# Order of a planned kernel: how many waiting tiles of the big pool a tile may pass, 2 to 6, and result stores without a due time

## The chip, the cores and the metric

The kernel runs on one core of one Trainium2 chip. Times are device microseconds (us) of one execution, as the device measures it; the median of the runs counts. Beside the timed runs there is one execution that the hardware profiler recorded, with each engine's instructions: TensorE (PE, matmuls), VectorE (DVE), ScalarE (ACT), GpSimd (POOL) and SyncE (SP, which issues DMAs).

## The reference

One layer of a streaming encoder on x of 1024 positions by 1024 channels, in float32. Cut to what matters:

```python
h = x @ w_in + b_in                      # 1024 x 6144
xa, za, xb, zb, ga, gb = split(h)        # six of 1024 channels
ya = rg_lru(causal_conv4(xa)) * silu(za) # gates by 16 blocks of 64x64, then a scan over time
yb = multi_scale_pool(xb) * silu(zb)     # running means over 2, 4, 8, 16 steps, then 4 blocks of 256x256
merged = sigmoid(ga) * (ya @ w_proj_a) + sigmoid(gb) * (yb @ w_proj_b)
x = layer_norm(2**0.25 * x + merged @ w_out + b_out) * gain + bias
```

In the scan, `h_t = a_t * h_{t-1} + u_t`, with `a = exp(-8 * r * softplus(-lambda))`: a vector softplus(-lambda) of 1024 numbers is needed once, before the first gate's exponential.

## The kernel before

**Tiling.** All is laid out with channels on the 128 partitions and time along the free axis. Each float32 operand of a matmul is split into a rounded high part (a cast on ACT) and the rest (a subtraction on DVE), and three matmuls of 128x512 (high by high, high by low, low by high) stand for one product: names end in `h` and `l`. The large products are done by a seven-product block scheme after Strassen and Winograd, whose sums of blocks DVE makes, or DMAs that add.

**Stages, by the trace's time.** From 0 to about 60 us a first part loads x and the first weights and does the groups `G0` and `A0` in an order of its own: the sums of x blocks are `t13`, `t24` (one buffer each for four quarters), their high and low parts are `x13h`, `x57h`, `x64h` and `x64l`, `xp0` is the first input of the convolution, and the softplus is a chain of DVE instructions on 128x8 with one exponential on ACT in it (lines 1070 to 1092, tiles `sp_y`, `sp_z`, `sp_z2`, `sp_acc`). From 60 to 404 us the groups A1, G2, A2, ... alternate: a group A makes eight channels' worth of xa and za, and its convolution `xc`, its split into `xch` and `xcl`, gates `ps_g`, `r`, `i`, and the scan follow two groups later. Then the groups B (xb, zb, pooling products `ps_pool`) until 511 us. From 511 to 675 us the merge: a list of 14 steps (`steps`, line 1164: a1, a2, a6, a5, a3, a7, a4, then b1, b2, b6, b7, b5, b4, b3), each four output tiles of twelve matmuls; the last pool product stands before a3. In step i the operands of step i+1 are cast (`cast`, line 1180: raw tiles such as `xb3r0`, `wb3r1` of step 13 become `oh13_0` to `oh13_3` on ACT and `ol13_0` to `ol13_3` on DVE) and those of step i+2 loaded (`load`, line 1170). What a step ends is multiplied by a gate, added into `m00`, `m20`, `m40`, ... and split on ACT and DVE (`split_m`, line 1213: `m000`, `m040` are high parts, `m100` low ones). From 675 us the last product `ps_o`, then the norm and the stores.

**What sets the order.** The code above only records tasks. `Plan.order` (line 253) then plays the kernel through with a table of costs and gives every task a start; the instructions are emitted in the order of these starts, all from line 387. PE and POOL keep the order in which the code records them; DVE, ACT and SP take, of the tasks whose inputs are there in the play, the one with the earliest due time, and the due time follows from when PE would need the result. What a task writes into must have a buffer: tiles with the same tag share a pool's buffers (`x`: 28 buffers of 128x1024, which hold x, its sums, and in the merge the `oh` and `ol`, gates and `m`; `w` 10, `r` 4, `k` 10, `e` 4). `slots` (line 282) hands them out in the order in which the code first writes the tiles, except that a tile may take a buffer ahead of some that still wait: it must stand among the first `AHEAD_OF[tag]` of the waiting tiles, and only if enough buffers are free for those ahead of it too. An SP task (a DMA) may not start earlier than 25 us before its due time (`LEAD`, line 36). On the chip each engine runs its instructions strictly in the order emitted, each when its semaphores allow.

Of the kernel before, what the change touches and what calls it, by code (L numbers as in the profile page):

```python
# [35 lines left out]
LEAD = 25.0  # L36
# [1 line left out]
SOON = 2.0  # L38
SHORT = ("ps", "e")
SHORT_LATEST = 1.0  # L40
AHEAD_OF = {"k": 6, "e": 2, "gr": 1, "x": 2}


C_BIN = 0
# [117 lines left out]
class Plan:  # L162
# [90 lines left out]
    def order(self):  # L253
        T = self.tasks
        for t in T:
            for j in t.deps:
                T[j].users.append(t.i)
        clock, pos = 1.5, []
        ideal = {}
        for t in T:  # L260
            if t.eng == "PE":
                ideal[t.i] = clock
                clock += t.time
            pos.append(clock)
        for t in reversed(T):
            short = t.eng != "PE" and any(r.tile.tag in SHORT for r in t.ins)
            t.due = ideal.get(t.i, pos[t.i] + (SHORT_LATEST if short else t.late))
            for u in t.users:
                t.due = min(t.due, T[u].due - t.wait)
        tags = {}  # L270
        for t in T:
            t.left, t.ready, t.start = len(t.deps), 0.0, None
            for s in t.new:
                if s.left == 0:
                    s.left = len(s.users)
                    tags.setdefault(s.tag, ([0.0] * s.pool.bufs, []))[1].append(s)
        free = {e: 0.0 for e in ("PE", "DVE", "ACT", "POOL", "SP")}
        waiting = {e: [] for e in free}
        pe = [t for t in T if t.eng == "PE"]
        state = {"table": None, "SP": 0.0, "POOL": 0.0, "pe": 0}  # L280

        def slots(t, now, commit=False):

            when = now
            for s in t.new:
                if not s.held:
                    times, queue = tags[s.tag]
                    ahead = queue.index(s)
                    if ahead >= AHEAD_OF.get(s.tag, 1) or len(times) <= ahead:
                        return None  # L290
                    when = max(when, sorted(times)[ahead])
                    if commit:
                        s.held = True
                        queue.remove(s)
                        times.remove(max((x for x in times if x <= now), default=min(times)))
            return when

        def begin(t, now):
            slots(t, now, True)
            if t.table and state["table"] not in t.table:  # L300
                now += 1.29
                state["table"] = min(t.table)
            t.start = now
            free[t.eng] = now + t.time
            if t.dma:
                state[t.eng] = max(now + t.time + 1.2, state[t.eng]) + t.dma
                t.end = state[t.eng] + 0.7
            else:
                t.end = now + t.wait
            for u in t.users:  # L310
                u = T[u]
                u.left -= 1
                u.ready = max(u.ready, now + t.time if u.eng == t.eng and not t.dma else t.end)
                if u.left == 0 and u.eng != "PE":
                    waiting[u.eng].append(u)
            for r in {x.tile: x for x in t.outs + t.ins}:
                r.left -= 1
                r.end = max(r.end, t.end)
                if r.left == 0 and r.tag and not r.pool.dram:
                    tags[r.tag][0].append(r.end)  # L320

        for t in T:
            if t.left == 0 and t.eng != "PE":
                waiting[t.eng].append(t)
        now, done = 0.0, 0
        while done < len(T):
            moved = True
            while moved:
                moved = False
                while state["pe"] < len(pe) and pe[state["pe"]].left == 0:  # L330
                    t = pe[state["pe"]]
                    when = slots(t, max(free["PE"], t.ready))
                    if when is None:
                        break
                    begin(t, when)
                    state["pe"] += 1
                    done += 1
                    moved = True
                for e in ("ACT", "DVE", "SP", "POOL"):
                    if free[e] > now:  # L340
                        continue
                    can, soon = [], []
                    for t in waiting[e]:
                        if t.chain is not None and T[t.chain].start is None:
                            continue
                        when = slots(t, max(now, t.ready, t.due - LEAD if e == "SP" else 0.0))
                        if when is None:
                            continue
                        if when <= now:
                            can.append(t)  # L350
                        elif when < now + 3.0:
                            soon.append((when, t))
                    if e == "ACT":
                        key = lambda t: (t.due + (SWITCH if t.table and state["table"] not in t.table else 0.0), t.i)
                    else:
                        key = lambda t: (t.due, t.i)
                    for t in sorted(can, key=key):
                        end = now + t.time + (1.29 if t.table and state["table"] not in t.table else 0.0)
                        if any(u.due < t.due and when < end and u.due < end - HOLD for when, u in soon):
                            continue  # L360
                        waiting[e].remove(t)
                        begin(t, now)
                        done += 1
                        moved = True
                        break
            times = [f for f in free.values() if f > now]
            for e in waiting:
                for t in waiting[e]:
                    if t.chain is not None and T[t.chain].start is None:
                        continue  # L370
                    when = slots(t, max(t.ready, t.due - LEAD if e == "SP" else 0.0))
                    if when is not None and when > now:
                        times.append(when)
            if done < len(T):
                if not times:
                    raise RuntimeError("stuck at %.1f: %s" % (now, [(t.op, t.args[0].tile.name if isinstance(t.args[0], Ref) else "", t.i) for e in waiting for t in waiting[e]][:20] + [[(k, len(v[0]), [s.name for s in v[1][:3]]) for k, v in tags.items()], T[pe[state["pe"]].i].args[0].tile.name]))
                now = min(times)
        return sorted(T, key=lambda t: (t.start, t.i))
# [21 lines left out]
def layer_kernel(ctx: ExitStack, tc: tile.TileContext, xq, x, w_in, par, wg, w_pool, wpa, wpb, w_out, rows, out):  # L400
# [206 lines left out]
    def load_group(i):  # L607
        w = weights_steps(i)
        for js in ("4", "75", "63 apart", "12") if i >= len(order) - 2 else ("12", "4", "75", "63"):
            w.step(js)  # L610
        return w.out
# [488 lines left out]
    weight_sums("a", wpa)  # L1100
    weight_sums("b", wpb)
    for i in range(1, len(order)):
        kind, c = order[i]
        if i + 1 < len(order):
            W[i + 1] = load_group(i + 1)
# [322 lines left out]
```

## Time and profile before

| | us |
|---|---|
| median of 3 runs (769.88, 773.46, 773.16) | 773.16 |
| the profiled execution | 771.97 |
| its span (first to last instruction) | 770.2 |
| PE busy | 749.9 |
| DVE busy | 602.6 |
| ACT busy | 432.4 |

A view of one engine's instructions in time gives for each row the start, the length, the engine, the line, the operation, what it writes and reads, and, in brackets, how long the engine was idle just before and whose result it waited for. Buffer numbers are left out of names there: `ol` stands for `ol9_1` as for `ol13_3`. Since line 387 emits everything, the line tells nothing; time and names do. Successive matmuls overlap: a row may be 0.39 long and the next starts 0.23 later. The granted clock (PEclk) is the share of full speed at which TensorE was let run in a stretch: 1.00 is 2.4 GHz, and the other of its two levels is 1.2 GHz.

### The profile page before, as it was taken

What the parts mean: (1) busy time and instruction counts of PE and PEld (TensorE: products, weight loads), DVE (VectorE), ACT (ScalarE), POOL (GpSimd) and SP (SyncE); (2) the same over time, 40 slices, a digit from 0 to 9 for tenths busy, and PEclk for the clock granted to TensorE, in tenths of its full rate; (3) what the DMA queues carried; (4) which work ended last, traced back from release to release, by engine and by line L of the source; (5) the groups of instructions that cost most, each with busy time, mean ns of one, the idle gap of its engine ahead of it and who ended that gap; (6) DMA issues with size and microseconds to landing.
All of it is one profiled execution on the core that took longest, in us unless ns stands there. A gap on an engine that the chain in (4) does not pass through costs nothing.

```text
span 770.2 us, 8752 instructions
## 1 busy us (share of the span) xinstructions
PE 749.9 (97%) x3308; PEld 610.6 (79%) x3308; DVE 602.6 (78%) x768; ACT 432.4 (56%) x556; POOL 36.3 (5%) x74
## 2 busy tenths in 40 slices
PE   8989999999999999999999999999999999899996
PEld 5868888888888888888878888888888877688885
DVE  5999686969696969696898678679658968978487
ACT  6657868777777868686755354464452655230000
POOL 0001010000000101000001101000000100000000
PEclk9989999999999999999999999999999999999998
DMA  8235764666476658352219849795699995262022
GB/s 300 86 112 151 202 165 139 184 170 167 178 176 166 168 162 218 132 178 82 69 54 206 152 123 255 247 323 198 219 295 304 339 288 185 91 251 104 27 84 110
DMA packets 54731, 135.91 MB, mean 176 GB/s; under 512 B 3936, under 2 KB 7136, under 8 KB 54624
## 3 DMA queue, kind: packets, MB, share of 16 engines
q1 hardware_dynamic: 41792, 99.69, 37.1%
q0 software_dynamic: 12896, 35.65, 21.3%
q8 instruction: 26, 0.43, 0.2%
q14 instruction: 17, 0.14, 0.0%
HBM read 114.36 MB, written 56.62 MB: 222 GB/s over the span
## 4 chain that ended last, share of the span: by engine, by line
PE 86%; DVE 9%; ACT 2%; DMA 1%; issue 1%; SPq 0%; DVEq 0%; ACTq 0%
PE ps_o L387 11%; PE a_A L387 10%; PE a_G L387 10%; PE a_B L387 7%; PE pa_a L387 6%; PE c_A L387 6%; PE pa_b L387 5%; PE c_G L387 5%; PE c_B L387 4%; PE ps_pool L387 3%; PE e_A L387 3%; PE pc_a L387 3%; PE pc_b L387 2%; PE e_G L387 2%; PE ps_s L387 2%; PE e_B L387 2%
## 5 line engine op out<-in xcount | busy, mean ns | idle before, releaser
L387 PE MATMUL ps_o<-woh,m 128*128 128x512 f32 (+1 forms) x272 | 80.3, 379 | 0.0
L387 ACT ACT_TABLE_LOAD x39 | 50.0, 1283 | 39.9 <-DVE mv L387 38.5
L387 PEld LDWEIGHTS ps_o<-woh,m 128*128 128x128 f32 x272 | 50.1, 188 | 9.9
L387 PE MATMUL ps_o<-wol,m 128*128 128x512 f32 (+1 forms) x136 | 51.5, 379 | 0.0
L387 DVE TENSOR_TENSOR i<-i,xc 128x1024 f32<-128x1024 f32 x8 | 9.8, 1226 | 45.3 <-ACT i L387 45.3
L387 DVE SCALAR_TENSOR_TENSOR xc<-xp,par_sb,xc 128x1024 f32<-128x1024 f32 x24 | 30.8, 1283 | 0.5
L387 PEld LDWEIGHTS ps_o<-wol,m 128*128 128x128 f32 x136 | 25.6, 188 | 4.9
L387 ACT ACTIVATE m<-m 128x512 fp32r<-128x512 f32 x16 | 9.8, 628 | 30.7 <-DVE m L387 30.7
L387 PE MATMUL pa_b<-oh,oh 128*128 128x512 f32 x64 | 25.1, 392 | 1.7 <-ACT oh L387 1.7
L387 PE MATMUL pa_b<-oh,ol 128*128 128x512 f32 x64 | 25.3, 395 | 0.5 <-DVE ol L387 0.5
L387 PE MATMUL pa_b<-ol,oh 128*128 128x512 f32 x64 | 25.1, 392 | 0.7 <-DVE ol L387 0.7
L387 DVE TENSOR_TENSOR z<-ps_o,z 128x512 f32<-128x512 f32 (+1 forms) x17 | 11.2, 659 | 17.9 <-PE ps_o L387 17.4
L387 PE MATMUL pa_a<-oh,ol 128*128 128x512 f32 x64 | 24.9, 389 | 0.0
L387 PE MATMUL pa_a<-oh,oh 128*128 128x512 f32 x64 | 24.9, 389 | 0.0
L387 PE MATMUL pa_a<-ol,oh 128*128 128x512 f32 x64 | 24.9, 389 | 0.0
L387 POOL COPY paced<-pace 128x1 f32<-128x1 f32 x19 | 8.3, 435 | 341.8 <-ACT pace L387 341.8
L387 ACT ACTIVATE r<-ps_g,par_sb 64x512 f32<-64x512 f32 x32 | 21.9, 683 | 2.5 <-PE ps_g L387 2.0
L387 PE MATMUL c_A<-x64h,wd_A 128*128 128x512 f32 x64 | 22.7, 417 | 0.0
L387 ACT ACTIVATE i<-ps_g,par_sb 64x512 f32<-64x512 f32 x32 | 21.9, 683 | 0.5
L387 ACT ACTIVATE sd<-mv,eps 128x1 f32<-128x1 f32 x8 | 2.4, 294 | 34.8 <-DVE mv L387 34.8
L387 PE MATMUL ps_pool<-mixh,wp 128*128 128x512 f32 x64 | 21.9, 415 | 0.0
L387 ACT ACTIVATE zb<-zb,par_sb 128x1024 f32<-128x1024 f32 (+1 forms) x16 | 14.9, 937 | 11.6 <-DVE zb L387 11.4
(434 smaller groups left out, 2378.0 us busy)
## 6 DMA issues: line engine op xcount, KB each, us to landing
sg<-sg SPq DMA_DIRECT2D x16, 512.0 KB, 3.5
ra_A<-in_w_in SPq DMA_DIRECT2D x8, 512.0 KB, 5.7
rb_A<-in_w_in SPq DMA_DIRECT2D x8, 512.0 KB, 4.3
ya<-r SPq DMA_DIRECT2D x8, 512.0 KB, 2.9
ra_B<-in_w_in SPq DMA_DIRECT2D x8, 512.0 KB, 3.4
rb_B<-in_w_in SPq DMA_DIRECT2D x8, 512.0 KB, 4.3
yb<-zb SPq DMA_DIRECT2D x8, 512.0 KB, 6.0
sgla<-sg SPq DMA_DIRECT2D x8, 512.0 KB, 7.6
```

The source lines that it names most:

```text
L387: getattr(getattr(nc, t.op[0]), t.op[1])(*a, **k)
```

## The change

Three lines of the planner. Of the tiles that wait for a buffer of the pool `x`, a tile that stands among the first six may now take one, where it was the first two. And DMAs whose result no other task reads are no longer held to 25 us before their due time; of all DMAs only the 16 stores of the result are such.

```diff
-AHEAD_OF = {"k": 6, "e": 2, "gr": 1, "x": 2}
+AHEAD_OF = {"k": 6, "e": 2, "gr": 1, "x": 6}
...
-                        when = slots(t, max(now, t.ready, t.due - LEAD if e == "SP" else 0.0))
+                        when = slots(t, max(now, t.ready, t.due - LEAD if e == "SP" and t.users else 0.0))
...
-                    when = slots(t, max(t.ready, t.due - LEAD if e == "SP" else 0.0))
+                    when = slots(t, max(t.ready, t.due - LEAD if e == "SP" and t.users else 0.0))
```

No instruction is added or taken away. PE and POOL keep their order row for row; DVE, ACT and SP are ordered anew in many places, the DMAs of SP only from its 109th row on (the loads of the merge), and the 16 stores of the result stand at the same rows as before. Three places:

**The softplus in the first part, on DVE** (`nps` is a small constant made in both; `sp_y` is the exponential that ACT writes; `xp0` reads the product `e_A0`). Before:

```order
L387 TENSOR_SCALAR nps_372<-par_sb_154 128x8
L387 SCALAR_TENSOR_TENSOR xp0_103<-e_A0_354,par_sb_154,m1_A0_358 128x512
L387 TENSOR_TENSOR wcl_A0_385<-ra_A0_125,wch_A0_374 128x1024
L387 SCALAR_TENSOR_TENSOR t24_0_393<-t13_0_225,xr0_0_87 128x512
L387 SCALAR_TENSOR_TENSOR t24_1_400<-t13_1_234,xr1_0_100 128x512
L387 SCALAR_TENSOR_TENSOR t24_2_407<-t13_2_312,xr2_0_113 128x512
L387 TENSOR_SCALAR sp_z_414<-sp_y_369 128x8
L387 RECIPROCAL sp_z_414<-sp_z_414 128x8
L387 TENSOR_TENSOR sp_z_414<-sp_z_414,sp_y_369 128x8
```

The same place of the changed kernel:

```order
L387 TENSOR_SCALAR nps_374<-par_sb_154 128x8
L387 TENSOR_SCALAR sp_z_378<-sp_y_326 128x8
L387 RECIPROCAL sp_z_378<-sp_z_378 128x8
L387 TENSOR_TENSOR sp_z_378<-sp_z_378,sp_y_326 128x8
L387 TENSOR_TENSOR sp_z2_383<-sp_z_378 128x8
L387 TENSOR_TENSOR sp_acc_98<-sp_acc_98,sp_z2_383 128x8
L387 TENSOR_SCALAR sp_acc_98<-sp_acc_98 128x8
...
L387 SCALAR_TENSOR_TENSOR xp0_103<-e_A0_357,par_sb_154,m1_A0_359 128x512
L387 TENSOR_TENSOR wcl_A0_397<-ra_A0_125,wch_A0_376 128x1024
L387 SCALAR_TENSOR_TENSOR t24_0_404<-t13_0_176,xr0_0_87 128x512
```

Nine of the chain's instructions, from the first that reads `sp_y` on, have moved from behind three sums `t24` to ahead of `xp0`; of the 13 that stood between the sum `t24_3` and the next `x64l0`, 11 are left.

**A turn of the A and G groups, on DVE** (`xc1` the convolution, `xcl1` its low part that the gate product reads, `xp2` the next group's input, which reads the product `e_A2`). Before:

```order
L387 TENSOR_TENSOR wbl_A2_959<-rb_A2_717,wbh_A2_941 128x1024
L387 SCALAR_TENSOR_TENSOR xc1_944<-xp1_599,par_sb_154,xc1_944 128x1024 x2
L387 TENSOR_TENSOR sg32_6_982<-c_G2_892,u2_G2_955 128x512
L387 TENSOR_TENSOR sg32_6_982<-a_G2_853,m7_G2_912 128x512
L387 SCALAR_TENSOR_TENSOR r0_756<-a0_832,i0_770 128x1024
L387 TENSOR_TENSOR xcl1_1012<-xc1_944,xch1_980 128x1024
L387 TENSOR_TENSOR ra_A2_676<-ra_A2_676 128x512
L387 MEMSET xp2_1022 128x3
L387 SCALAR_TENSOR_TENSOR xp2_1022<-e_A2_1007,par_sb_154,m1_A2_1009 128x512
L387 TENSOR_TENSOR r0_756<-r0_756,z0_530 128x1024
L387 TENSOR_TENSOR wcl_A2_1041<-ra_A2_676,wch_A2_1025 128x1024
```

The same place of the changed kernel:

```order
L387 MEMSET xp2_969 128x3
L387 TENSOR_TENSOR sg32_6_973<-c_G2_892,u2_G2_953 128x512
L387 TENSOR_TENSOR wbl_A2_978<-rb_A2_717,wbh_A2_959 128x1024
L387 TENSOR_TENSOR ra_A2_684<-ra_A2_684 128x512
L387 TENSOR_TENSOR sg32_6_973<-a_G2_847,m7_G2_912 128x512
L387 SCALAR_TENSOR_TENSOR xc1_945<-xp1_589,par_sb_154,xc1_945 128x1024 x2
L387 TENSOR_TENSOR r0_756<-r0_756,z0_540 128x1024
L387 SCALAR_TENSOR_TENSOR xp2_969<-e_A2_1010,par_sb_154,m1_A2_1012 128x512
L387 TENSOR_TENSOR xcl1_1037<-xc1_945,xch1_1018 128x1024
L387 TENSOR_TENSOR wcl_A2_1044<-ra_A2_684,wch_A2_989 128x1024
```

`xcl1` has moved from ahead of `xp2`, with the scan `r0<-a0,i0` before it, to right behind `xp2`; the scan now stands further up. The like is found in each of the seven turns.

**The end of the merge, on ACT** (`oh13_0` to `oh13_3` are the four high parts of the last step, b3; `m041`, `m040`, `m060` are high parts of results of step b4 and before it, which wait for DVE's sums). Before:

```order
L387 ACTIVATE m041_5155<-m41_4576 128x512 x2
L387 CAST oh12_3_5177<-wb4r1_4978 128x1024
L387 CAST oh13_0_5189<-xb3r0_5046 128x1024
L387 ACTIVATE m040_5200<-m40_4703 128x512
L387 CAST oh13_1_5204<-xb3r1_5070 128x1024
L387 CAST oh13_2_5218<-wb3r0_5145 128x1024
L387 ACTIVATE m040_5200<-m40_4703 128x512
L387 ACTIVATE m060_5265<-m60_4733 128x512
L387 CAST oh13_3_5269<-wb3r1_5193 128x1024
```

The same place of the changed kernel:

```order
L387 CAST oh12_3_5094<-wb4r1_4983 128x1024
L387 ACTIVATE m041_5138<-m41_4583 128x512
L387 CAST oh13_0_5144<-xb3r0_4994 128x1024
L387 ACTIVATE m041_5138<-m41_4583 128x512
L387 CAST oh13_2_5168<-wb3r0_5098 128x1024
L387 CAST oh13_1_5175<-xb3r1_5015 128x1024
L387 CAST oh13_3_5203<-wb3r1_5120 128x1024
L387 ACTIVATE m040_5213<-m40_4692 128x512 x2
L387 ACTIVATE m060_5253<-m60_4786 128x512
```

`oh13_3` has moved up past two `m040` and one `m060`. **In step b2, on DVE** (`ol9_0` to `ol9_3` are the low parts for step b6; `m1_b0` to `m1_b3` its results on their way into `m00` and `m20`). Before:

```order
L387 TENSOR_TENSOR m1_b1_4748<-m1_b1_4748,sglb2_0_4719 128x512
L387 TENSOR_TENSOR m00_4175<-m00_4175,m1_b1_4748 128x512
L387 SCALAR_TENSOR_TENSOR m100_4864<-m00_4175,m000_4847 128x512
L387 TENSOR_TENSOR m1_b2_4776<-pe_b2_4851,m1_b2_4776 128x512
L387 SCALAR_TENSOR_TENSOR ol9_2_4876<-wb6r0_4612,oh9_2_4822 128x1024
L387 TENSOR_TENSOR m1_b2_4776<-m1_b2_4776,sglb2_1_4721 128x512
L387 TENSOR_TENSOR m20_4214<-m20_4214,m1_b2_4776 128x512
L387 TENSOR_TENSOR m1_b3_4807<-pe_b3_4870,m1_b3_4807 128x512
L387 TENSOR_TENSOR ol9_1_4900<-xb6r1_4690,oh9_1_4812 128x1024
L387 TENSOR_TENSOR m1_b3_4807<-m1_b3_4807,sglb2_1_4721 128x512
L387 TENSOR_TENSOR m20_4214<-m20_4214,m1_b3_4807 128x512
L387 SCALAR_TENSOR_TENSOR ol9_3_4915<-wb6r1_4636,oh9_3_4878 128x1024
```

The same place of the changed kernel:

```order
L387 TENSOR_TENSOR ol9_0_4771<-xb6r0_4626,oh9_0_4736 128x1024
L387 TENSOR_TENSOR m60_4786<-um_a2_4304,sgla4_1_4606 128x512
L387 TENSOR_TENSOR m60_4786<-um_a3_4325,sgla4_1_4606 128x512
L387 TENSOR_TENSOR ol9_1_4799<-xb6r1_4633,oh9_1_4782 128x1024
L387 SCALAR_TENSOR_TENSOR ol9_2_4821<-wb6r0_4577,oh9_2_4814 128x1024
L387 TENSOR_TENSOR m1_b0_4745<-pe_b0_4824,m1_b0_4745 128x512
L387 TENSOR_TENSOR m1_b0_4745<-m1_b0_4745,sglb2_0_4641 128x512
L387 TENSOR_TENSOR m00_4181<-m00_4181,m1_b0_4745 128x512
L387 TENSOR_TENSOR m1_b1_4773<-pe_b1_4845,m1_b1_4773 128x512
```

`ol9_1` and `ol9_2` have moved up from among the instructions on `m1_b2` and `m1_b3` to ahead of all on `m1_b0`. The casts of the earlier steps have moved in the same direction.

## Rows read from the trace of the kernel before

**Rows 1.** Page, engines: busy us (share of the span) and instructions.

```profile
PE 749.9 (97%) x3308; PEld 610.6 (79%) x3308; DVE 602.6 (78%) x768; ACT 432.4 (56%) x556; POOL 36.3 (5%) x74
```

**Rows 2.** PE's waits by what was awaited: us in total, times, longest.

```profile
PE a_A L387 <- DVE x64l L387: 3.1, 1, 3.1
PE ps_pool L387 <- DVE mixl L387: 2.6, 2, 1.9
```

**Rows 3.** Busy us by engine (PE, PEld, DVE, ACT, POOL) and PEclk, by stretch.

```profile
50.00:75.00 25.00, 25.00 (x97) 20.06 (x98) 23.60 (x39) 15.22 (x19) 2.35 (x3) 0.88 0.51 168
60.00:400.00 340.00, 340.00 (x1534) 277.44 (x1533) 271.21 (x317) 254.50 (x323) 21.91 (x36) 1.00 0.54 155
```

**Rows 4.** PE in time, first part: start, length, operation, idle before.

```profile
49.86 0.80 PE L387 MATMUL a_A<-x64l,wch_A 128*128 128x512 f32 x1 [3.10 <-DVE x64l L387]
50.88 0.63 PE L387 MATMUL c_A<-x64h,wd_A 128*128 128x512 f32 x1
```

**Rows 5.** DVE in time, first part.

```profile
36.44 0.75 DVE L387 SCALAR_TENSOR_TENSOR xp<-e_A,par_sb,m_A 128x512 f32<-128x512 f32 x1 [1.20 <-PE e_A L387]
...
40.04 0.17 DVE L387 TENSOR_SCALAR sp_z<-sp_y 128x8 f32<-128x8 f32 x1
...
44.78 0.16 DVE L387 TENSOR_TENSOR sp_acc<-sp_acc,sp_z 128x8 f32<-128x8 f32 x1
...
47.23 0.17 DVE L387 TENSOR_TENSOR sp_acc<-sp_acc,sp_z 128x8 f32<-128x8 f32 x1
...
49.12 0.69 DVE L387 TENSOR_TENSOR x64l<-t,x64h 128x512 fp32r<-128x512 f32 x1
```

**Rows 6.** ACT in time, first part.

```profile
33.65 0.59 ACT L387 COPY m_A<-a_A 128x512 f32<-128x512 f32 x1 [0.43 <-PE a_A L387]
...
36.23 1.28 ACT L387 ACT_TABLE_LOAD   x1
...
37.52 0.21 ACT L387 ACTIVATE sp_y<-sp_y 128x8 f32<-128x8 f32 x1
```

**Rows 7.** DVE in time, one turn of groups A and G.

```profile
115.46 1.20 DVE L387 TENSOR_TENSOR xcl<-xc,xch 128x1024 fp32r<-128x1024 f32 x1
...
118.17 0.75 DVE L387 SCALAR_TENSOR_TENSOR xp<-e_A,par_sb,m_A 128x512 f32<-128x512 f32 x1 [0.89 <-PE e_A L387]
```

**Rows 8.** PE in time, the same turn.

```profile
121.04 0.40 PE L387 MATMUL ps_g<-xcl,gh 64*128 64x512 f32 x2
```

**Rows 9.** PE in time, merge.

```profile
616.17 0.39 PE L387 MATMUL pa_b<-oh,oh 128*128 128x512 f32 x1
617.23 0.50 PE L387 MATMUL pa_b<-ol,oh 128*128 128x512 f32 x1 [0.67 <-DVE ol L387]
...
655.45 0.50 PE L387 MATMUL pc_b<-oh,ol 128*128 128x512 f32 x1 [0.80 <-DVE ol L387]
...
668.06 0.50 PE L387 MATMUL pa_b<-oh,oh 128*128 128x512 f32 x1 [1.71 <-ACT oh L387]
...
669.32 0.50 PE L387 MATMUL pa_b<-oh,ol 128*128 128x512 f32 x1 [0.52 <-DVE ol L387]
```

**Rows 10.** DVE in time, merge.

```profile
615.96 1.21 DVE L387 TENSOR_TENSOR ol<-xb6r,oh 128x1024 fp32r<-128x1024 f32 x1
...
654.18 1.22 DVE L387 TENSOR_TENSOR ol<-wb4r,oh 128x1024 fp32r<-128x1024 f32 x1
```

**Rows 11.** ACT in time, merge.

```profile
650.10 0.63 ACT L387 ACTIVATE m<-m 128x512 fp32r<-128x512 f32 x1 [7.74 <-DVE m L387]
...
666.45 0.63 ACT L387 ACTIVATE m<-m 128x512 fp32r<-128x512 f32 x1 [2.85 <-DVE m L387]
666.98 1.03 ACT L387 CAST oh<-wb3r 128x1024 fp32r<-128x1024 f32 x1
```

**Rows 12.** SP's issues in time, merge.

```profile
602.66 0.36 SPq L387 DMA_DIRECT2D xb7r<-t3b  x1
```

**Rows 13.** The tile xb7r: its loads' time to landing.

```profile
DMA to landing us min/median/max: 12.7/13.2/13.6
```

## The prediction

> **What bounds the kernel now.** The page's engine rows come first: PE is busy for 749.9 of the 770.2 us of the span, DVE for 78% of it [rows 1]. PE's matmuls are the same before and after, in the same order, so the time can only move by PE's idle stretches, by the granted clock, and by the head and the tail. The list of PE's waits says which idle stretches there are. The largest is one of 3.1 us for an `x64l` from DVE, in the first part; pooling products wait 2.6 us in two places [rows 2]. The others that matter lie in the merge, four of them, and PE's rows there show each: 0.67, 0.80, 1.71 and 0.52, together 3.70 us [rows 9]. Each costs more than its bracket, since the first matmul after it is 0.50 long, where the one before it is 0.39 (616.17 and 617.23 in [rows 9]): 4 x 0.11 = 0.44. The merge's waits are thus worth 4.1 us. Between 60 and 400 us PE is busy throughout, at full clock [rows 3]. So the change can win 4.1 us in the merge, may win or lose in the first part, and can only lose in the groups.
>
> The wait in the first part has a second price. After it the granted clock is down: 0.88 is the mean of 50 to 75 us [rows 3], and matmuls take 0.63 [rows 4]. With two levels, 1.2 and 2.4 GHz, a mean of 0.88 over 25 us is (1 - 0.88) x 2 x 25 = 6 us at the lower level. The engine had been idle for 3.10 us before that.
>
> **The second edit** frees the 16 stores of the result from their due time, and none of them changes its row on SP. It costs and gives nothing.
>
> **First part: cost 0.85 us.** DVE stands still for 1.20 us before `xp0` at 36.44 [rows 5]. The planner now puts nine instructions of the softplus there. On the chip they cannot run there: they read `sp_y`, which ACT writes. ACT's copy of m1 starts at 33.65 and takes 0.59; its table load for the exponential takes 1.28 and the exponential 0.21 [rows 6]. In the changed order these three follow each other at once, so `sp_y` is there at 33.65 + 0.59 + 1.28 + 0.21 = 35.7 (37.7 before). The chain's step is (47.23 - 44.78) / 12 = 0.204 [rows 5], so nine take 1.84, and `xp0`, behind them, starts at about 35.8 + 1.84 = 37.7 instead of 36.44: 1.26 late. From there to the `x64l` for which PE waits, DVE has the same work but two chain steps fewer (11 instead of 13 before `x64l0`): -0.41. That `x64l` then starts at 49.12 + 0.85 = 49.97 [rows 5], and PE waits 0.85 longer. Nothing hides it: PE is waiting there already.
>
> How the clock takes a longer wait is shown by no row. From below: the low stretch ends at the same moment, then 0.85 us less of it falls on matmuls, which gives back half, and the cost is 0.4. From above: the low stretch lasts half as long again, 3 us more, half of which is lost, and the cost is 0.85 + 1.5 = 2.4. I take the same 6 us, as after the wait that is there, and keep 0.4 to 2.4.
>
> One rule speaks for a higher cost. In the trace the exponential starts at 37.52, and the table load before it ends at 36.23 + 1.28 = 37.51 [rows 6]: nothing lies between. The Trainium skill, page "ScalarE: Activation LUTs", section "What ACT_TABLE_LOAD costs", gives 1283 ns for the load and about 1380 ns more for a drain with each switch. The first figure agrees with the row, the second this row does not show; by it the first part would cost about 2.2 us (an estimate from that page) and the whole come to 771.5.
>
> **Groups A and G: no cost.** In each of seven turns `xcl`, the low part that the gate product reads, now stands behind the next `xp` instead of ahead of it. That `xp` waits for PE (0.89 before it) and starts at 118.17; `xcl` follows 0.68 later, at 118.85, and takes 1.20: done at 120.05 [rows 7]. The matmul that reads it starts at 121.04 [rows 8]. It has 1.0 us to spare. The scan, which now stands further up, gives DVE the time to have the rest of the convolution done before that `xp`.
>
> **Pooling: nothing.** Around both pooling waits [rows 2] the order is as before.
>
> **Merge: -4.1 us, and 0.2 back.** All four waits have one form: a cast or a low part for the next step stands behind instructions that finish the present one. The first is for `ol9_1`, 615.96 to 617.17, and the second for `ol12_3`, 654.18 to 655.40 [rows 10]. `ol12_3` was late because its high part on ACT stands behind `m041`, which waited 7.74 us for DVE's sum until 650.10. `oh13_3` is the worst: it starts at 666.98 behind `m060` at 666.45, which again waited for DVE [rows 11], and PE's third and fourth waits are for it and for its low part. In the new order `ol9_1` and `ol9_2` stand ahead of all the evacuations of step b2, and `oh13_3` ahead of `m040` and `m060`. Since casts of the steps before also move up, raw buffers come free earlier and SP's loads go out earlier. `oh12_3` can be cast where ACT falls idle, at 650.10 - 7.74 = 642.4 [rows 11], 9.5 us sooner, so `ol12_3` is there about 10 us before PE wanted it (655.45 - 0.80 = 654.65, [rows 9]). Walking on with the durations of before, the raw buffer that `ol12_3` frees gets `wb3r1` soon after, `oh13_3` is cast at about 650, and `ol13_3` is ready at about 656, 10 us before PE first stood still for it (668.06 - 1.71 = 666.35, [rows 9]). Four waits gone: -4.1.
>
> What comes next is a chain on ACT in step b6. The cast `oh10_0` now stands ahead of `m000`, and has to wait for the load of `xb7r`; that load is behind an addition by DMA that no reordering moves, takes 12.7 to 13.6 us to land [rows 13], and the second was issued at 602.66 [rows 12], so the data can be there only at about 602.66 + 13.2 = 615.9. Behind it on ACT come `m000` and `oh10_1`, then on DVE `m100`, m1_b3 and `ol9_3`, and by my walk `ol9_3` ends 0.7 to 2 us before PE wants it. Bounds: 0 if the landing is like the median, 2.4 us if it is two low parts (1.21 each, [rows 10]) late. I take 0.2, near the lower end.
>
> The product with w_out and the tail keep their order: nothing.
>
> **Sum,** against the profiled execution: 771.97 + 0.85 - 4.1 + 0.2 = 768.9. That execution was 1.19 below the median of the runs (773.16), so in the frame of the median: 770.1.
>
> **The rivals.**
>
> *Waits for loads take the place (C).* The chain on ACT above is late by the whole 2.4 us. For it: the loads of `xb7r` land late and spread over 0.9 us. Against it: it was not late before, and the casts ahead of it are done earlier. 770.1 - 0.2 + 2.4 = 772.3.
>
> *The table switch takes longer than its row (T).* Something as long as the load itself (1.28, [rows 6]) lies between load and exponential once the exponential follows a copy directly. Against it: 37.51 to 37.52. 770.1 + 1.28 = 771.4. The drain that the Trainium skill gives on the page named above would be such a thing.
>
> *The change does not do what it says (D).* A buffer that the planner believes free is free later on the chip, casts in the new order wait for loads as long as they waited for sums, and the four waits stay; the first part still pays. For it: the planner's DMA times are a model, and DMAs are dense in this stretch. Against it: two of the four waits are behind sums on ACT, in front of which the casts now stand, with their raw tiles long landed. 773.16 + 0.85 + 0.2 = 774.2.
>
> *The groups pay seven times (E), slower than before.* `xcl` has 1.0 us to spare in my walk. If two more instructions of its size (1.20, [rows 7]) come between `xp` and `xcl` in time, because the scan or the product with the silu is done later than I have it, each turn loses 2.4 - 1.0 = 1.4: 770.1 + 7 x 1.4 = 779.9. The kernel becomes slower than 773.16 from 0.44 us a turn on, that is, with `xcl` 1.5 us later than I have it. For it: seven copies of one margin. Against it: DVE stood still before that `xp`, so up to there it has slack.
>
> **How the numbers follow.** A measurement of this kernel tells about 0.5% from no change, 3.9 us: faster is below 769.3, slower above 777.0. Forecast 0.66; C 0.09; T 0.04; D 0.10; E 0.11. The forecast lies 0.8 above the bound for faster, and the unknown terms (first part 0.4 to 2.4, chain 0 to 2.4) and the runs' own spread (769.88 to 773.46) put it on either side, half and half: 0.33 faster, 0.33 same. C, T and D are within 0.5%: same 0.33 + 0.09 + 0.04 + 0.10 = 0.56; slower is E, 0.11. The range: below, the forecast less 2.7, as a run as far under the median as most of the spread (773.16 - 769.88 = 3.3) would give: 767.4. Above, D with 0.6 for its spread: 774.8. Outside lie E and some 0.06 of the rest.
>
> **What would show it.** In the trace after: the wait for `x64l` is 3.9 to 4.0 us instead of 3.1, and `xp0` starts at 37.7 with `sp_y` as what it was held by; PEclk of 50 to 75 stays at 0.86 to 0.88. PE's waits for `oh` and `ol` in the merge are below 0.5 us together; the pooling waits stay at 2.6. `xcl` of a turn ends at least 0.5 us before its matmul. I am wrong in the merge if waits for `oh` or `ol` remain near 617, 655 or 667, or a new one stands near 620 to 626 (C); wrong in the groups if `ps_g` appears among PE's waits, seven times (E); wrong in the first part if the wait for `x64l` is over 5 us or PEclk of 50 to 75 below 0.83.

## The result, and the profile after

The changed kernel takes 765.47 us in the median (765.15 to 767.53), the one before 772.63 in the same comparison: a ratio of 0.9921, 95% interval 0.9897 to 0.9945. That is 7 us, where 3 were forecast, and below the low end of the range (767.4). The profiled execution took 765.47, with a span of 763.7, against 771.97 and 770.2 before: 6.5 us less.

PE's waits by what was awaited, kernel after (us in total, times, longest):

```profile
PE a_A L387 <- DVE x64l L387: 3.3, 1, 3.3
PE ps_pool L387 <- DVE mixl L387: 2.6, 2, 1.9
...
PE c_A L387 <- DVE x64l L387: 0.9, 1, 0.9
```

Against [rows 2], the first wait is 3.3 instead of 3.1 (3.9 to 4.0 were forecast), the pooling waits are the same 2.6, and a second wait for an `x64l` of 0.9 is new. No wait for an `oh` or `ol` is left: the merge's four waits [rows 9] are gone.

Since PE's instructions stand in the same order, the start of the same matmul in both traces tells where time was won. The table gives the first matmul of a block in each; the last column is what changed since the row above.

| start of the block | before | after | after less before | step |
|---|---|---|---|---|
| a_A, first part | 30.73 | 30.89 | +0.16 | +0.16 |
| a_G, after the waits for x64l | 56.20 | 56.50 | +0.30 | +0.14 |
| a_B, after the first pooling product | 409.27 | 408.01 | -1.26 | -1.56 |
| pc_b of step b7 | 626.66 | 624.35 | -2.31 | -1.05 |
| pa_b of step b3 | 660.57 | 656.99 | -3.58 | -1.27 |
| ps_o | 674.45 | 667.88 | -6.57 | -2.99 |

The merge gives 5.3 us, the first part costs 0.14, and 1.56 come from a place where the wait has not changed. The first step, 0.16, says nothing: over the 14 profiled executions of this document that block starts anywhere from 29.9 to 30.9, over the four of the kernel before from 30.2 to 30.9. Busy time by stretch shows what it is (columns as in [rows 3]: PE, PEld, DVE, ACT, POOL, then PEclk). Kernel before:

```profile
400.00:425.00 25.00, 23.12 (x95) 18.48 (x94) 20.23 (x28) 13.94 (x18) 3.22 (x3) 0.93 0.83 193
650.00:675.00 25.00, 21.96 (x94) 17.00 (x93) 23.04 (x33) 9.46 (x13) 0.00 (x0) 1.00 0.39 126
```

Kernel after:

```profile
50.00:75.00 25.00, 23.59 (x96) 19.09 (x97) 23.08 (x33) 15.21 (x19) 2.35 (x3) 0.93 0.51 169
400.00:425.00 25.00, 23.12 (x101) 18.68 (x100) 20.88 (x29) 14.81 (x19) 3.17 (x3) 1.00 0.79 187
650.00:675.00 25.00, 25.00 (x111) 20.63 (x110) 23.74 (x37) 9.12 (x13) 0.00 (x0) 1.00 0.19 58
```

After the first pooling wait the granted clock was 0.93 before and is 1.00 now, with PE's busy time equal (23.12): the wait stayed, the low clock behind it did not come. In 50 to 75 us the clock is 0.93, not the 0.88 of [rows 3] or the 0.86 to 0.88 that was forecast. In 650 to 675 us PE is busy throughout, where it had 21.96 of 25.

The first part, DVE after, which answers to [rows 5]:

```profile
35.94 0.17 DVE L387 TENSOR_SCALAR sp_z<-sp_y 128x8 f32<-128x8 f32 x1 [1.55 <-ACT sp_y L387]
...
37.69 0.75 DVE L387 SCALAR_TENSOR_TENSOR xp<-e_A,par_sb,m_A 128x512 f32<-128x512 f32 x1
...
49.79 0.69 DVE L387 TENSOR_TENSOR x64l<-t,x64h 128x512 fp32r<-128x512 f32 x1
...
55.19 0.68 DVE L387 TENSOR_TENSOR x64l<-t,x64h 128x512 fp32r<-128x512 f32 x1
```

ACT after, which answers to [rows 6]:

```profile
33.81 0.59 ACT L387 COPY m_A<-a_A 128x512 f32<-128x512 f32 x1 [1.77 <-PE a_A L387]
34.40 1.28 ACT L387 ACT_TABLE_LOAD   x1
35.70 0.21 ACT L387 ACTIVATE sp_y<-sp_y 128x8 f32<-128x8 f32 x1
```

The chain's first reader of `sp_y` starts at 35.94, `xp0` at 37.69, both within 0.15 of the prediction (35.8, 37.7). The `x64l` that PE waits for starts at 49.79, 0.67 later than before, where 0.85 were forecast; 0.16 of it is there already at a_A.

A turn of the groups after, which answers to [rows 7, 8], DVE and then PE:

```profile
118.45 0.75 DVE L387 SCALAR_TENSOR_TENSOR xp<-e_A,par_sb,m_A 128x512 f32<-128x512 f32 x1 [1.17 <-PE e_A L387]
119.12 1.22 DVE L387 TENSOR_TENSOR xcl<-xc,xch 128x1024 fp32r<-128x1024 f32 x1
```

```profile
121.33 0.39 PE L387 MATMUL ps_g<-xcl,gh 64*128 64x512 f32 x2
```

`xcl` ends at 119.12 + 1.22 = 120.34, 1.0 us ahead of its matmul, as worked out.

The merge after, DVE and then ACT, which answers to [rows 10, 11]:

```profile
599.57 1.23 DVE L387 TENSOR_TENSOR ol<-xb6r,oh 128x1024 fp32r<-128x1024 f32 x1
...
638.76 1.22 DVE L387 TENSOR_TENSOR ol<-wb4r,oh 128x1024 fp32r<-128x1024 f32 x1
...
655.08 1.22 DVE L387 TENSOR_TENSOR ol<-wb3r,oh 128x1024 fp32r<-128x1024 f32 x1
```

```profile
605.98 1.05 ACT L387 CAST oh<-xb7r 128x1024 fp32r<-128x1024 f32 x1 [0.23 <-DMA xb7r<-t3b]
...
610.04 1.05 ACT L387 CAST oh<-xb7r 128x1024 fp32r<-128x1024 f32 x1 [1.72 <-DMA xb7r<-t3b]
...
646.63 1.05 ACT L387 CAST oh<-wb3r 128x1024 fp32r<-128x1024 f32 x1
```

`ol9_1` is done at 600.8 (617.2 before), `ol12_3` at 640.0 (655.4), `oh13_3` at 647.7 (668.0) and `ol13_3` at 656.3 (669.3). ACT does wait for the loads of `xb7r`, 0.23 and 1.72 us, as the rival C had it; PE does not feel it.

The second edit: with it alone, and two tiles to pass, the order of all five engines is row for row that of before; with the first edit alone it is that of the changed kernel. So it has no part in the result.

### The profile page after: what moved, and what is told of

It is laid out like the page before. It is cut to its first block, busy times and chain, and to the rows that moved or that the text cites. A ratio compares the mean times of both kernels' runs of the same rounds, so it can differ in the third digit from the quotient of the medians.

```text
span 763.7 us, 8776 instructions
## 1 busy us (share of the span) xinstructions
PE 746.5 (98%) x3308; PEld 609.3 (80%) x3308; DVE 603.7 (79%) x768; ACT 433.9 (57%) x556; POOL 37.7 (5%) x74
## 4 chain that ended last, share of the span: by engine, by line
PE 87%; DVE 9%; DMA 1%; ACT 1%; issue 1%; SPq 1%; DVEq 0%
PE ps_o L387 12%; PE a_G L387 10%; PE a_A L387 10%; PE a_B L387 9%; PE pa_b L387 6%; PE pa_a L387 6%; PE c_A L387 5%; PE c_G L387 5%; PE c_B L387 4%; PE pc_a L387 3%; PE pc_b L387 3%; PE ps_pool L387 3%; PE e_B L387 2%; PE e_A L387 2%; PE e_G L387 2%; PE ps_g L387 2%
## 5 line engine op out<-in xcount | busy, mean ns | idle before, releaser
L387 PEld LDWEIGHTS ps_o<-wol,m 128*128 128x128 f32 x136 | 25.6, 188 | 5.0
L387 PE MATMUL c_B<-x64h,wd_B 128*128 128x512 f32 x64 | 21.0, 389 | 0.0
```

What stands on the lines that cost most here:

```text
L387: getattr(getattr(nc, t.op[0]), t.op[1])(*a, **k)
```

## The experiments

Times before are given as measured beside each group of runs: 771.99 (23 executions) for the first four, 771.95 for the next four, 771.68 for the last four. What a ratio's interval means in us is worked out with these.

**The two kernels once more.** Nothing is edited; the question is the granted clock.

> The kernel before once more, unchanged, for the granted clock. Theory A (the low-clock stretches fall differently in each execution): PE's waits are the same within 0.2 us, but the stretch after the first pooling wait (400 to 425 us) or the one after the wait for x64l (50 to 75 us) comes out at another clock than in the first profile (0.93 and 0.88), and the times spread over 2 to 4 us in steps of about 1.7. Theory B (the clock follows from the order of the instructions): both stretches come out as in the first profile within 0.01, and the times spread by under 1 us.

> The changed kernel once more, unchanged. Theory A: the first pooling wait is again followed by a stretch at the lower clock in some executions (0.93 in 400 to 425 us instead of 1.00), times from 765 to 768. Theory B: 1.00 in 400 to 425 us and 0.93 in 50 to 75 us again. In both: no wait for oh or ol in the merge.

Before again: 772.33 (771.17 to 774.07, 12 executions). After again: 765.60 (764.45 to 766.85), ratio 0.9916 (0.9899 to 0.9933), 6.5 us. In the merge and at the pooling products PE's waits are those of the first two profiled executions; in the first part the kernel before now has a second wait for `x64l`, of 1.0, which its first profiled execution did not have. The clock differs too. The kernel before, second profiled execution, by stretch:

```profile
400.00:425.00 25.00, 23.11 (x102) 18.85 (x102) 20.90 (x29) 14.31 (x18) 3.02 (x3) 1.00 0.85 203
665.00:670.00 5.00, 3.72 (x9) 2.71 (x10) 4.22 (x6) 2.39 (x4) 0.00 (x0) 0.69 0.01 3
```

The low clock after the pooling wait is missing here as it is in the kernel after; instead there is one in the merge. PE there:

```profile
665.76 0.50 PE L387 MATMUL pa_b<-oh,oh 128*128 128x512 f32 x1 [1.71 <-ACT oh L387]
...
667.01 0.80 PE L387 MATMUL pa_b<-oh,ol 128*128 128x512 f32 x1 [0.52 <-DVE ol L387]
667.61 0.63 PE L387 MATMUL pa_b<-oh,oh 128*128 128x512 f32 x1
668.03 0.63 PE L387 MATMUL pa_b<-ol,oh 128*128 128x512 f32 x1
```

Right behind the third and the fourth wait (1.71 and 0.52) the matmuls take 0.63, as in [rows 4], and so until 670.2. In the first profiled execution of this kernel, the one the prediction rests on, the same place ran at full clock:

```profile
665.00:670.00 5.00, 2.76 (x11) 1.66 (x11) 4.69 (x8) 2.62 (x4) 0.00 (x0) 1.00 0.00 0
```

The second profiled execution of the kernel after has full clock after the pooling wait (1.00) and 0.66 in 50 to 55 us, as the first. So theory B falls for the kernel before: the same instructions meet different clocks from one execution to the next.

**Only the merge, only the first part.** The number of tiles that may be passed depends on the planner's time.

```diff
-                    if ahead >= AHEAD_OF.get(s.tag, 1) or len(times) <= ahead:
+                    if ahead >= (6 if s.tag == "x" and now > 470.0 else AHEAD_OF.get(s.tag, 1)) or len(times) <= ahead:
```

(`e_merge`; in `e_first` the condition is `now < 60.0`. The buffers taken up to then also bring the new order of the groups.)

> Six waiting tiles may be passed only from 470 us of the planner's time on; the order up to the end of the groups is that of before. If the merge's four waits with their restarts and three shorter hitches are the gain: 5.2 us faster than before, 767.4 against 772.6 (767 to 768). If the gain needs the new order of the first part for the clock: 768.5 to 769.5, that is 3.5 to 4 us.

> Six waiting tiles may be passed only up to 60 us of the planner's time; the new order of the first part and of the groups, the merge as before. By the sum on record: 0.85 us slower than before, with the merge's four waits in place. If the clock follows from the order (theory B): 1.3 us faster than before, from -1.56 us after the first pooling wait and +0.3 in the first part. If it does not (theory A): 0 to 1 us slower, and the clock of 400 to 425 us may be 0.93 or 1.00.

`e_merge`: 764.42 (763.95 to 765.71), ratio 0.9904 (0.9889 to 0.9920): 7.4 us faster, 6.2 to 8.6. `e_first`: 772.61 (771.40 to 774.73), ratio 1.0013 (1.0001 to 1.0025): 1.0 us slower, 0.1 to 1.9. The first part's price (0.85 forecast, 0 to 1 by theory A) lies within the interval of `e_first`, which only just leaves out no change at all. The merge alone brings all of the gain, but both expectations for `e_merge` missed: 7.4 us is more than the 5.2 that PE's rows give for its waits. `e_first`, which keeps the merge's waits, shows the low clock behind them again:

```profile
665.00:670.00 5.00, 3.13 (x8) 2.21 (x9) 4.69 (x7) 2.83 (x5) 0.00 (x0) 0.72 0.00 0
```

**Parts of the merge.** Six tiles may be passed from 470 to 630 us of the planner's time (`e_early`), or from 640 on (`e_late`); the edit is that of `e_merge` with these bounds.

> Six waiting tiles may be passed from 470 to 630 us of the planner's time: the merge's first two waits (for ol9_1 and ol12_3) go, the third and fourth (for oh13_3 and ol13_3) stay, and so does all before the merge. Theory A, a low-clock stretch worth about 1.5 us hangs on the third and fourth wait in most executions: only the two waits' own 1.1 + 1.3 us and a hitch are won, 2.3 to 2.6 us, and the times spread as widely as those of before (over 3 us). Theory C, every wait of the merge brings its share of clock loss: 3.5 us or more are won.

> Six waiting tiles may be passed only from 640 us of the planner's time on: the third and fourth wait go, and the second may go, the first stays. Theory A: 3.0 us for the third and fourth wait, 1.3 for the second if it goes, and 1.0 to 1.5 of clock on the mean of the executions: 5 to 6 us faster than before, with 665 to 670 us at full clock in every look, and a spread under 3 us. Theory C: 3 to 4.3 us faster.

`e_early`: 765.94 (764.86 to 766.69), ratio 0.9913 (0.9897 to 0.9928), 6.7 us faster. `e_late`: 765.71 (765.27 to 767.56), ratio 0.9917 (0.9898 to 0.9935), 6.4 us. The expectations for `e_early` can't be told apart by its time, since the premise of both failed: it lost all four waits. (The "3.5 us or more" of theory C is met by that, not by C's reason.) In its order `oh13_3` still stands behind `m040` and `m060`; on the chip these came sooner. ACT in `e_early`:

```profile
660.71 0.63 ACT L387 ACTIVATE m<-m 128x512 fp32r<-128x512 f32 x1 [2.07 <-PE pa_b L387]
661.24 1.03 ACT L387 CAST oh<-wb3r 128x1024 fp32r<-128x1024 f32 x1
```

DVE, the low part `ol13_2` and the last sum that ACT waits for ahead of `oh13_3`, in the kernel before:

```profile
659.79 1.22 DVE L387 TENSOR_TENSOR ol<-wb3r,oh 128x1024 fp32r<-128x1024 f32 x1
...
665.72 0.69 DVE L387 TENSOR_TENSOR m<-m,um_b 128x512 f32<-128x512 f32 x1
```

The same two instructions in `e_early`:

```profile
654.82 1.22 DVE L387 TENSOR_TENSOR ol<-wb3r,oh 128x1024 fp32r<-128x1024 f32 x1
...
659.92 0.69 DVE L387 TENSOR_TENSOR m<-m,um_b 128x512 f32<-128x512 f32 x1
```

The step b3 began at 657.79 there and `oh13_3` is cast 3.4 us into it; in the kernel before it was 666.98 - 660.57 = 6.4 us. The same instructions stand ahead of it in both. What differs is DVE: `ol12_0` to `ol12_2` are done by 637 in `e_early`, and in the kernel before they lie between 643.8 and 648.9, among the sums that ACT's `m` wait for; `ol13_2` is done 1.8 us before b3 begins, and in the kernel before 0.4 us after; the sum starts 2.1 us into b3 instead of 5.2, one other sum, on `c_b`, having moved behind it. So the last two waits came of a backlog on DVE, and with the earlier casts it is gone. The first two waits and the last two are not separate items, and my reading of the last two from the row just ahead of `oh13_3` was too short. `e_late` keeps the first wait and loses the other three, as its one remaining row says:

```profile
PE pa_b L387 <- DVE ol L387: 0.7, 1, 0.7
```

Its PE rows gain 1.24 + 3.00 = 4.2 us in the merge, and the times 6.4 (5.0 to 7.9). Theory C (3 to 4.3) misses; theory A's 5 to 6 lies within the interval, and its other two signs came: 665 to 670 us at 1.00, and a spread under 3 us (2.3).

**How often the clock falls.** Two more profiled executions of the kernel before, nothing edited.

> The kernel before, one more look at the granted clock. Theory A (a low-clock stretch of about 3.4 us follows the merge's third and fourth wait in most executions, and the pooling wait in some): 665 to 670 us at about 0.7 if PE's waits there are 1.7 and 0.5 again. Theory B (such a stretch comes at random places, waits or not): low stretches elsewhere, with no wait just ahead of them.

> As the look before. Theory A: 665 to 670 us at about 0.7 in most of the four looks at the kernel before, and 1.00 from 60 to 400 us, where PE does not wait, in all.

771.22 and 771.83 us. The third profiled execution and the fourth, same stretch:

```profile
665.00:670.00 5.00, 3.76 (x11) 2.70 (x12) 4.17 (x6) 2.34 (x4) 0.00 (x0) 0.79 0.01 3
```

```profile
665.00:670.00 5.00, 3.16 (x9) 2.26 (x10) 4.69 (x7) 2.83 (x5) 0.00 (x0) 0.81 0.01 3
```

(0.79 and 0.81, not the 0.7 of the expectation, because the low stretch begins about 1 us later than in before2 and runs on past 671.) So of five profiled executions of kernels with the merge's third and fourth wait, four have a low stretch right behind them (all but the one that I predicted from), and of nine of kernels without these waits, none has. Behind the pooling wait, which is in all 14, two have one. In all ten with over 3 us of waiting for the first `x64l`, one follows within the next 6 us. Theory A holds; what decides in which execution the clock falls, no run shows. In four of four the stretch in the merge cost 1.5 to 1.65 us in PE's rows: the step from a_B to ps_o grew by 1.50, 1.61, 1.65 (before2, before3, before4) and 1.55 (`e_first`) against the first profiled execution.

The runs' record has the mean granted clock of the other executions too, and it says the same. Among the 14 above, the one without a low stretch between matmuls has 0.998, those with one 0.995 or 0.996, with two 0.993 or 0.994, and the first of the kernel before, with one of 6.8 us and one of 3.4, 0.991. By this number the 23 executions of the kernel before fall into steps: 2 at 0.995 took 769.7 and 770.0 us, 13 at 0.993 or 0.994 took 771.1 to 773.1, 8 at 0.989 to 0.991 took 772.7 to 773.9. Most of its spread goes with the clock. The mean is 0.9927 for the kernel before (these and the 12 of before2), 0.9947 for the changed kernel (11) and 0.9957 for `e_merge` (6). Taken times the span that is, as an estimate, 1.5 us less lost to the clock with the change and 2.3 us less in `e_merge`: with the 5.3 of the merge's rows 7.6, where `e_merge` measured 7.4.

**The softplus chain elsewhere.** First, the changed kernel with the chain kept back (`e_sp`), and the same with six tiles only from 470 us on (`e_spm`):

```diff
-            t.left, t.ready, t.start = len(t.deps), 0.0, None
+            t.left, t.ready, t.start = len(t.deps), 0.0, None; t.ready = 60.0 if t.outs and t.outs[0].tile.name == "sp_nl" else 0.0
```

> The changed kernel with the softplus chain kept back until 60 us of the planner's time, so that it stands behind all of the first part's x64l. Theory A, the chain on DVE is what PE waits for there (22 of its instructions, 4.5 us, stand before the x64l): both waits for x64l (3.3 and 0.9) go or fall under 0.5 together, the clock stays up there, and the time is 5 to 6 us below the changed kernel's, near 760. Rival: PE waits for x64l because of the casts on ACT or the sums on DVE as well; then 1.5 to 3 us are left of the waits, the clock falls as before, and the time is 762.5 to 764.

> As e_merge (six only from 470 us on), with the softplus chain kept back until 60 us. If the 1 us that the new order of the first part costs is the chain ahead of xp0 and nothing else, this and e_sp are within 0.5 us of one another, near 760. If the rest of the new order of the first part and the groups costs too, this one is faster by about 1 us.

`e_sp`: 764.75 (764.54 to 766.37), ratio 0.9905 (0.9888 to 0.9923), neither the 760 that was expected nor the 762.5 to 764 of its rival. PE's waits:

```profile
PE c_A L387 <- DVE x64l L387: 2.0, 1, 2.0
...
PE ps_g L387 <- DVE xcl L387: 1.4, 1, 1.4
```

The first wait for `x64l` is gone (3.3), the second has grown from 0.9 to 2.0, and a new one of 1.4 has come: the chain now stands ahead of the first turn's `xcl`, its last part on DVE without a gap from 75.99 to 78.58, and the gates wait for it.

```profile
75.99 0.16 DVE L387 TENSOR_TENSOR sp_acc<-sp_acc,sp_z 128x8 f32<-128x8 f32 x1
...
78.58 0.74 DVE L387 SCALAR_TENSOR_TENSOR xp<-e_A,par_sb,m_A 128x512 f32<-128x512 f32 x1
79.24 1.21 DVE L387 TENSOR_TENSOR xcl<-xc,xch 128x1024 fp32r<-128x1024 f32 x1
```

This is the mechanism of the rival E, at one turn and brought on by my own edit. `e_spm`: 766.91 (765.35 to 767.54), ratio 0.9924 (0.9910 to 0.9939); neither expectation holds. The two profiled executions lie 2.3 us apart: in that of `e_spm` a low clock stands behind the pooling wait (1.6 us), and 0.7 are lost behind the start of ps_o. Why the tail takes longer stays open.

Then the chain off DVE (`e_gp`): 22 of its instructions go to GpSimd (the expectation says 20), idle there, and the last three on DVE are kept back until 60 us.

```diff
-    nc.vector.tensor_tensor(z, z, y, ALU.mult)
+    nc.gpsimd.tensor_tensor(z, z, y, ALU.mult)
...
-        nc.vector.tensor_tensor(acc, acc, z2, ALU.mult)
-        nc.vector.tensor_scalar(acc, acc, 2.0 / n, None, ALU.add)
+        nc.gpsimd.tensor_tensor(acc, acc, z2, ALU.mult)
+        nc.gpsimd.tensor_scalar(acc, acc, 2.0 / n, None, ALU.add)
```

> The changed kernel with 20 instructions of the softplus chain moved from DVE to GpSimd (and the last three on DVE kept back until 60 us of the planner's time): ACT's and SP's order stay those of the changed kernel. If DVE's chain is what holds the first part: the first wait for x64l (3.3) goes, the second is at most the 2.0 of e_sp, no wait of ps_g for xcl appears, and the time is 763 +- 0.7, 2 to 3 us below the changed kernel's. Rival: GpSimd's small instructions slow DVE's or hold up the gates: above 765.

> The same with six waiting tiles passed only from 470 us of the planner's time on. If the new order of the first part and the groups costs nothing beside the chain: within 0.5 us of e_gp. If it costs in itself: up to 1 us faster than e_gp.

`e_gp`: 764.07 (762.00 to 765.72), ratio to before 0.9902 (0.9879 to 0.9924). `e_gpm`, with six tiles from 470 us on: 763.42 (762.00 to 764.13), ratio 0.9889 (0.9867 to 0.9911), 8.6 us faster than before and the lowest median of all. The 763 +- 0.7 expected for `e_gp` missed, and so did its rival. The two are not told apart, and their intervals overlap that of the changed kernel (0.9899 to 0.9933): a gain over it is not shown by the times. PE's waits in `e_gp`:

```profile
PE c_A L387 <- DVE x64l L387: 2.0, 1, 2.0
...
PE a_A L387 <- DVE x64l L387: 0.6, 1, 0.6
```

The first wait falls from 3.3 to 0.6, no `ps_g` waits, and in this execution the clock is up from 50 to 75 us (1.00). PE's rows are 3.5 us ahead of the changed kernel's at the end of the first part (53.02 against 56.50; 0.5 of it they had at a_A) and stay so; in the median 1.5 of it is left, for its executions spread from 762.0 to 765.7. The profiled one is the fastest and the only one with a mean granted clock of 0.998; the others have 0.993 to 0.996, and the two slowest 0.993. `e_gpm`'s profiled execution has 0.93 in 50 to 75 us.

## Why the prediction was wrong

**Which way, and how much.** The mechanism in the merge was right and the direction too; what the forecast had wrong is the price of the merge's waits, above all the clock behind them. The sum said -3.05 us for the profiled pair, and it came to -6.5. By its own steps:

- **The merge, -4.1: mis-sized.** It measured -5.3 in PE's rows. Two things were left out. Each wait costs more than its bracket at both ends: 616.17 to 617.23 is 1.06, where two matmuls are otherwise 0.23 apart, so 0.83 is lost before the restart and 0.11 behind it, against 0.67 + 0.11 in my sum; over four waits 0.65. Three more hitches have no bracket at all, because they are shorter than a matmul's modelled length. The one at the start of b3, kernel before, PE:

```profile
660.79 0.39 PE L387 MATMUL pa_b<-ol,oh 128*128 128x512 f32 x1
661.06 0.50 PE L387 MATMUL pa_b<-oh,ol 128*128 128x512 f32 x1
661.40 0.39 PE L387 MATMUL pa_b<-oh,oh 128*128 128x512 f32 x1
```

  Here 0.27 and 0.34 stand where 0.23 and 0.23 should be: 0.15 us, three times. Those are in no list of waits, and only the start times show them. Together 4.1 + 0.65 + 0.45 = 5.2.
- **The clock behind the merge's waits: the step that failed.** The prediction priced a low clock behind the first part's wait and none behind the merge's third and fourth, since the one execution it read had none there. The term stood at nothing. In four of five profiled executions there is one, worth 1.5 to 1.65 us. With it the merge is worth 5.3 + 0.8 x 1.6 = 6.6 us on the mean; `e_merge` gives 7.4 (6.2 to 8.6). By the terms as measured the change is worth 6.6 less 0.5 for the first part, 6.1 us; the two comparisons gave 7 and 6.5 (5.2 to 7.8).
- **The frame.** The profiled execution of before had a low clock in another place, behind the pooling wait, and a longer one in the first part, which the one of after did not have. Its total was near the median nevertheless, so the sum against its own time looked safe. Of the 6.5 us between the two profiled executions 1.56 are this difference, and the change has no part in it; in the mean of many executions the merge's own low clock takes its place.
- **The first part, +0.85: right in kind, too large, and hidden in the profiled pair.** `sp_y`, `xp0` and the chain came as worked out, the `x64l` 0.67 later instead of 0.85, and 0.51 counted from a_A. PE's wait grew by 0.2 only, since the last matmul ahead of it came 0.4 later too. From a_A to a_G the changed kernel takes 25.6 us in both its profiled executions; before2, before3 and before4, with a low stretch as long, take 25.1: the price is 0.5 us. `e_first` gives +1.0 (0.1 to 1.9). In the profiled pair only +0.14 shows, because the low clock of the kernel before was longer there. How that works is told by the second wait: DVE's next `x64l` ends at 55.19 + 0.68 = 55.87. With the clock low for 6.8 us PE reaches it late and does not wait (before); with a shorter low stretch it waits 0.9 (after), with none so far 2.0 (`e_merge`). DVE sets the end of this part, and a low clock that is over by then costs little; in `e_merge` it came later, from 55 us on, fell on a_G, and cost 1.3 us there (a_G to e_G). PE in `e_merge`:

```profile
55.01 0.66 PE L387 MATMUL c_A<-x64l,wd_A 128*128 128x512 f32 x1 [2.02 <-DVE x64l L387]
...
56.32 0.63 PE L387 MATMUL a_G<-x13l,wah_G 128*128 128x512 f32 x1
```

  My bounds for the clock (0.4 to 2.4) took PE as what sets it.
- **The chain on ACT in step b6, +0.2: nothing.** ACT waits 1.72 us for the second `xb7r`, and `ol9_3` is still in time.
- **Groups, pooling, tail: as forecast.** `xcl` keeps its 1.0 us, the pooling waits are 2.6, `ps_o` to the end takes 95.8 us in both.

**The rivals.** T falls: the table load ends at 34.40 + 1.28 = 35.68 and the exponential starts at 35.70; the drain of about 1380 ns that the Trainium skill gives (page "ScalarE: Activation LUTs", section "What ACT_TABLE_LOAD costs") does not show in this row either, nor ahead of the load, which starts where the copy before it ends (33.81 + 0.59 = 34.40). C and D did not come; E did not come in the changed kernel and showed its price, 1.4 us for one turn, in `e_sp`.

**The range.** It was made from the unknown terms that I had named and from the runs' spread. The low end left out that the merge's term could be larger than the sum of its brackets. Had it held the 1.2 us of starts, stops and hitches, and one low stretch of 1.6 us behind the third and fourth wait, it would have reached 767.4 - 1.2 - 1.6 = 764.6. No row that the prediction had shows a low stretch in the merge; [rows 4] did show one behind a wait.

## What to carry to other kernels

A wait of the tensor engine cost here its bracket, about 0.27 us more for stopping and starting, and in some executions a stretch at half clock behind it; price all three wherever a wait may go, also where the one trace at hand shows full clock. Count start-to-start distances, since hitches shorter than a matmul's length are in no list. When an engine of small instructions is late again and again at the end of a stage, take its backlog as one item: moving early work forward cleared two waits in `e_early` whose own instructions did not move.

## What the runs showed of the hardware

- Low stretches of the granted clock between PE's matmuls were 3.4 us long wherever a profiled execution has one, read from the granted clock microsecond by microsecond, and once 6.8 (first execution of before, 49.3 to 56.1). They stood, from 10 us on, only behind waits of PE: within 6 us behind one of over 3 us in all 10 executions that have it (in `e_merge` and `e_early` only behind the second wait, of 2.0, with full clock between the two), behind one of 2.0 in the first part with none of over 3 ahead of it in 3 of 4 (`e_sp`, `e_spm`, `e_gpm`; not `e_gp`), behind 1.7 and 0.5 us close together in 4 of 5, behind one of 1.9 us in 2 of 14, behind the 1.4 and 1.5 for `xcl` in `e_sp` and `e_spm` in none, behind waits of under 1 us alone in the merge in none. The same kernel meets different sets of them from one execution to the next, and most of the spread of the kernel before (769.7 to 773.9 over 23 executions) goes with the mean granted clock (0.995 to 0.989). The kernels without the merge's waits spread by 1.8 to 2.4 us, `e_gp` by 3.7, over 4 to 6 executions each.
- GpSimd took 0.20 to 0.58 us, once 1.11, for an element-wise instruction on 128x8 in `e_gp`, and 11.1 us for its 22 of the chain (35.99 to 47.06), where DVE's chain runs at 0.20 a step. There it cost PE nothing: the first gate product starts at 77.6.
